# A pooled and RWKV-7 mixing block: the diagonal blocks of the score matrices gathered by ScalarE, chunk by chunk, and transposed by one contiguous VectorE instruction in place of two strided ones

## The chip, the cores and the metric

The kernel runs on one core of a Trainium2 chip. The metric is the device time of one execution in microseconds (us), taken as the median of several runs. The engines of the core are named as the profile names them: PE is TensorE (matmuls; PEld are its weight loads), DVE is VectorE, ACT is ScalarE, POOL is GpSimd, SP issues DMAs.

## The reference

`x` is (1, 4096, 1024), and everything is float32. Cut to what matters here:

```
h  = rmsnorm(x) * (1 + scale) + shift               # adaLN from c @ w_ada
p  = h @ w_in                                       # one projection for both branches
pool branch: trailing-window means (2, 4, 8, 16) minus the token, a small matmul, a SiLU gate
RWKV-7 branch, 512 channels, 8 heads of 64: r, w, k, v, a, z from p, each mixed with the token before
    kk = l2-normalised k * k_k
    S_t = S_{t-1} (diag(decay_t) - kk_t^T (a_t * kk_t)) + v_t^T k_t ;  y_t = S_t r_t
    y = groupnorm(y) + bonus, times a SiLU gate
out = rmsnorm(x + gate * (concat(pool, rwkv) @ w_out))
```

The recurrence over 4096 tokens is computed in chunks of 64 tokens. Within a chunk the state update of all tokens at once needs the inverse of a unit triangular 64x64 matrix, for each head.

## The kernel before, in words

Phase 1 (the first 440 us) computes the modulation, `h` and the pool branch. Phase 2 has 16 blocks, b = 0 to 15, of 256 tokens: 4 chunks (NCH) of 64 tokens times 8 heads (NH) make 32 instances (NI) of the triangular problem per block. For each block the program runs three functions:

- `scores(b)`: per chunk `ch`, PE multiplies BK with AR into two PSUM tiles (L659), and DVE multiplies these with a mask into `sc` (L666). `sc` is 128 partitions x 32 instances x 128 floats, so that the same element of two neighbouring instances lies 128 floats (512 bytes) apart.
- `inverse(b)`: the 64x64 matrix of each instance has two 32x32 blocks on its diagonal (rows 0 to 31 and rows 32 to 63). Both are brought with the instance in the partition and inverted there for all 32 instances at once. L703 transposes them into `Ab` (partitions 0 to 63), L704 multiplies by the norms `d2T`, L705 copies to partitions 64 to 127 (ACT), L707 copies to `W`; then come 30 back-substitution steps of two DVE instructions each, `Wt` = W * Ab (L721) and W += Wt (L726); L737 multiplies by `d2T` again ("W*d2T"); two transpositions (L739) write the result into `MT`, which is the lower 64 partitions of the tile `UV`; L740 transposes a part into `MQ` (DVE), L741 copies another (ACT). Then PE makes the off-diagonal block of the inverse: the products `qp` (L750), copies of them (L752), and a second set of products (L758). All DVE steps named here stand in `tc.high_priority(offset=PRI)`.
- `chain(b)`: the four chunks one after the other with the state S; L833 (`Sd`) is its first DVE instruction.

`front(b+1)` is the next block's projection: 17 segments named lo, then kS, rS, vS, zS for each of four pairs of heads. A segment is 8 times three matmuls into a PSUM tile `pj` (L552 to L554; f16 weights and activations in a high and a low part), an ACT eviction (L556) and a DVE eviction (L557). Between the segments lie small steps: `pl` and `pa` (L583, L584) with the activations `tw` and `ta`, the scan `L` (L591), `vps` (L624, copied by ACT into UV, L630) and `pb` (L637, used by DVE as `bon`, L638). `pj`, `pl`, `pa`, `vps` and `pb` share one pool of three PSUM banks in turn: each waits until what used its bank three allocations before has been read. `front` is a generator; `fill(n)` runs n of its steps at the places where `scores`, `inverse` and `chain` call it, so PE has the projection's matmuls among the others. In block 15 there is no next block, and from its inverse on `fill` runs `project`, the output projection (`po`, L947 to L949).

The Tile framework orders the instructions of each engine by priority and by its own estimates; each engine then executes its own list in order, and an instruction that waits holds up all that stand behind it. Some matmuls are pinned to program order.

Of the kernel before, what the change touches and what calls it, by code (L numbers as in the profile page):

```python
# [24 lines left out]
NH = 8  # L25
# [27 lines left out]
def kernel(  # L53
# [29 lines left out]
    V, A, G, PE, SP = nc.vector, nc.scalar, nc.gpsimd, nc.tensor, nc.sync  # L83
# [56 lines left out]
    with ExitStack() as ph:  # L140
# [179 lines left out]
        for tok in plan.split():  # L320
            op, q = tok[0], int(tok[1:] or 0)
# [158 lines left out]
    with ExitStack() as ph:  # L480
# [165 lines left out]
        def scores(b, f, fill):  # L646
            AR, BK = f["AR"], f["BK"]

            d2 = sm.tile([64, NI], F32, tag="d2", name=f"d2_{b}")
            d2T = sm.tile([P, 32], F32, tag="d2T", name=f"d2T{b}")  # L650
            sc = blk.tile([P, NI, P], F32, tag="sc", name=f"sc{b}")
            BT = blk.tile([P, NCH, 512], F32, tag="BT", name=f"BT{b}")
            for ch in range(NCH):

                pts = [pool.tile([P, 512], F32, tag=tg, name=f"scp{b}_{ch}_{tg}") for pool, tg in ((ps_sc, "sc"), (ps_x, "px"))]
                for j in range(4):
                    for hq in range(2):
                        o = 64 * hq
                        PE.matmul(  # L659
                            pts[hq][:, j * P : (j + 1) * P],  # L660
                            BK[o : o + 64, j, ch].rearrange("q a t -> q (a t)"),
                            AR[o : o + 64, j, ch].rearrange("q a t -> q (a t)"),
                            start=True, stop=True,
                        )
                for hq in range(2):
                    V.tensor_mul(  # L666
                        sc[:, ch * NH : (ch + 1) * NH, :].rearrange("q (j h) t -> q j h t", h=2)[:, :, hq],
                        pts[hq].rearrange("q (j t) -> q j t", j=4),
                        mask.unsqueeze(1).to_broadcast([P, 4, P]),
                    )  # L670
                fill(FS + 1)
                if ch == 2:
                    pt = ps_sc.tile([P, 512], F32, tag="sc", name=f"d2p{b}")
                    for c_ in range(NCH):
                        PE.transpose(pt[:64, c_ * P : (c_ + 1) * P], ssb[:, c_ * C : (c_ + 1) * C], ident)
                    V.tensor_scalar_max(
                        d2.rearrange("q (c p h) -> q c p h", c=NCH, h=2),
                        pt[:64].rearrange("q (c p e) -> q c p e", c=NCH, e=32)[:, :, :, 0:2], L2_EPS * L2_EPS,
                    )
                    V.reciprocal(d2, d2)  # L680
                    for g in range(2):
                        V.transpose(d2T[64 * g : 64 * g + 64], d2)
                if ch in (0, 3):
                    f["todo"].pop(0)()
                fill(FS)
                if ch % 2 == 0:
                    run(gns[0], 1)
            f["sc"], f["BT"], f["d2T"] = sc, BT, d2T

        def inverse(b, f, fill):  # L690

            fi = iter(FI)
            sc, d2T = f["sc"], f["d2T"]
            MT = f["UV"][0:64].rearrange("q c (h t) -> q (c h) t", h=NH)

            Ab = blk.tile([P, 32, 32], F32, tag="Ab", name=f"Ab{b}")
            W = blk.tile([P, 16, 32], F32, tag="W", name=f"W{b}")
            with tc.high_priority(offset=PRI):  # L700
                for kb in range(2):
                    o = 32 * kb
                    V.transpose(Ab[o : o + 32], sc[o : o + 32, :, o : o + 32].rearrange("s i t -> s t i"))  # L703
                V.tensor_mul(Ab[0:64], Ab[0:64], d2T[0:64].unsqueeze(2).to_broadcast([64, 32, 32]))  # L704
                A.copy(Ab[64:128], Ab[0:64])  # L705
                for g in range(2):
                    V.tensor_copy(W[64 * g : 64 * g + 64], Ab[0:64].rearrange("q (t g) s -> q t g s", g=2)[:, :, g, :])  # L707
            fill(next(fi))
            BK, BT = f["BK"], f["BT"]
            for ch in range(NCH):  # L710
                pt = ps_sc.tile([P, 512], F32, tag="sc", name=f"btp{b}_{ch}")
                for p in range(NPAIR):
                    PE.transpose(pt[:, p * P : (p + 1) * P], BK[:, p, ch].rearrange("q a t -> q (a t)"), ident)
                A.copy(BT[:, ch, :], pt)
                fill(FE)
            for k in range(30, 0, -1):
                r0 = (k + 1) // 2
                n = 16 - r0
                tmp = blk.tile([P, 16, 32], F32, tag="Wt", name=f"Wt{b}_{k}")
                with tc.high_priority(offset=PRI):  # L720
                    V.tensor_mul(  # L721
                        tmp[:, :n, :k],
                        W[:, r0:, k : k + 1].to_broadcast([P, n, k]),
                        Ab[:, k : k + 1, :k].to_broadcast([P, n, k]),
                    )
                    V.tensor_add(W[:, r0:, :k], W[:, r0:, :k], tmp[:, :n, :k])  # L726
                if k % 2 == 0:
                    fill(next(fi))
            Wf = W.rearrange("q t c -> q (t c)")
            MQ = blk.tile([P, NI, 32], F32, tag="Ab", name=f"MQ{b}")  # L730
            with tc.high_priority(offset=PRI):
                for kb in range(2):
                    for g in range(2):
                        q0 = 64 * g + 32 * kb
                        o = Wf[q0 : q0 + 32, g : g + 1]
                        G.memset(bass.AP(tensor=o.tensor, offset=o.offset, ap=[list(o.ap)[0], [34, 16]]), 1.0)
                V.tensor_mul(W, W, d2T.unsqueeze(1).to_broadcast([P, 16, 32]))  # L737
                for g in range(2):
                    V.transpose(MT[:, :, 0:32].rearrange("c i (t g) -> c g t i", g=2)[:, g], W[64 * g : 64 * g + 64])  # L739
                V.transpose(MQ[0:32], MT[0:32, :, 0:32])  # L740
                A.copy(MT[32:64, :, 32:64], MT[32:64, :, 0:32])  # L741
                G.memset(MT[32:64, :, 0:32], 0.0)
            fill(FT)
            f["px"] = [ps_x.tile([P, 512], F32, tag="px", name=f"px{b}_{hf}") for hf in range(2)]
            run(lead(b, f, 0))
            pt = ps_sc.tile([P, 512], F32, tag="sc", name=f"qp{b}")
            for j in range(8):
                for q in range(4):
                    i = 8 * q + j
                    PE.matmul(pt[32 * q : 32 * q + 32, j * 32 : (j + 1) * 32], sc[0:32, i, 32:64], MQ[0:32, i, :], start=True, stop=True)  # L750
            for q in range(4):
                A.copy(MQ[32:64, 8 * q : 8 * q + 8, :], pt[32 * q : 32 * q + 32, 0:256].rearrange("t (i c) -> t i c", c=32))  # L752
            fill(FQ)
            pt = ps_sc.tile([P, 512], F32, tag="sc", name=f"m21p{b}")
            for j in range(8):
                for q in range(4):
                    i = 8 * q + j
                    PE.matmul(pt[32 * q : 32 * q + 32, j * 32 : (j + 1) * 32], MQ[32:64, i, :], MT[32:64, i, 32:64], start=True, stop=True)  # L758
            for q in range(4):
                A.copy(MT[0:32, 8 * q : 8 * q + 8, 32:64], pt[32 * q : 32 * q + 32, 0:256].rearrange("c (i t) -> c i t", t=32))  # L760
# [3 lines left out]
        def ordered(mm):  # L764

            pin[0] = True
            return tc.keep_in_program_order(mm)
# [22 lines left out]
        def chain(b, f, fill):  # L790
            AR, UV, sc, BT, pc = f["AR"], f["UV"], f["sc"], f["BT"], f["pc"]
            MT = UV[0:64].rearrange("q c (h t) -> q (c h) t", h=NH)
            pe, po = f["px"]
            uo = 4 * HS
            for ch in range(NCH):
# [39 lines left out]
                for h in range(NH):  # L835
                    o, e = 64 * (h % 2), slice(h * HS, (h + 1) * HS)
                    ordered(PE.matmul(
                        psn[o : o + 64, (h // 2) * HS : (h // 2 + 1) * HS], BT[:, ch, e], UV[:, ch, e],
                        start=True, stop=True, skip_group_check=True,
# [70 lines left out]
        def run(g, n=100000):  # L910
            for _ in range(n):
                if next(g, run) is run:
                    return
# [51 lines left out]
        for b in range(NB2):  # L965
            f = fs[b]
# [80 lines left out]
```

## Time and profile before

| | |
|---|---|
| median of 3 runs | 2123.24 us (2123.21 to 2123.97) |
| the profiled execution | 2123.65 us, of which its span is 2121.9 us |
| TensorE clock granted, mean of the span | 0.982 of full |
| busy: PE, DVE, ACT, POOL | 1984.5, 1449.5, 965.5, 131.6 us |
| share of the chain that ended last: PE, DVE, ACT | 54%, 28%, 11% |

The busy time of an engine is what it spends in its own instructions. The chain that ended last is followed back from the last instruction to what released each step; its shares say on which engine the time to the end went.

### The profile page before, as it was taken

How to read it: one execution, taken by the hardware profiler on the slowest of the kernel's cores; microseconds unless marked ns; L12 is line 12 of the kernel's file. 1: busy time of each engine (PE TensorE's matmuls, PEld its weight loads, DVE VectorE, ACT ScalarE, POOL GpSimd, SP SyncE). 2: the span in 40 equal slices, each digit the busy share in tenths (PEclk: the TensorE clock that was granted, in tenths of full speed). 3: DMA queues.
4: the chain of work that ended last, by engine and by line, in shares of the span. 5: the costliest groups of instructions: out<-in, count | busy, mean ns of one | idle time of the engine just before them, and what ended most of it. 6: DMA issues, size and time to landing. Idle time of an engine off the chain costs nothing.

```text
span 2121.9 us, 48336 instructions
## 1 busy us (share of the span) xinstructions
PE 1984.5 (94%) x20186; PEld 1463.6 (69%) x20186; DVE 1449.5 (68%) x3549; ACT 965.5 (46%) x2119; POOL 131.6 (6%) x262
## 2 busy tenths in 40 slices
PE   5999999999999999999999999999999989999998
PEld 2444444677777777777777777777777767788886
DVE  7898987566857768578577686786776866533333
ACT  3545433345455554554555545545555453312111
POOL 0000000000000000000000100000000000100000
PEclk8999999999999999999999999999999999999999
DMA  8867767200110110101101101011011434443431
GB/s 304 278 224 239 243 217 269 66 21 2 31 27 7 31 26 7 32 2 31 27 7 31 27 6 32 2 31 27 6 32 27 134 111 140 157 142 130 153 105 70
DMA packets 140445, 183.19 MB, mean 86 GB/s; under 512 B 12098, under 2 KB 94018, under 8 KB 140227
## 3 DMA queue, kind: packets, MB, share of 16 engines
q1 hardware_dynamic: 140226, 180.11, 26.0%
q8 instruction: 158, 2.59, 0.5%
q14 instruction: 61, 0.49, 0.1%
HBM read 121.22 MB, written 58.85 MB: 85 GB/s over the span
## 4 chain that ended last, share of the span: by engine, by line
PE 54%; DVE 28%; ACT 11%; issue 4%; DMA 2%; POOL 0%; SPq 0%; DVEq 0%; ACTq 0%; POOLq 0%
PE po L947 6%; PE po L949 5%; PE po L948 5%; PE pj L552 5%; PE pj L554 4%; PE pj L553 4%; DVE W L726 4%; DVE Wt L721 4%; PE pp L412 4%; PE pp L411 4%; PE pp L410 4%; DVE Ab L703 3%; PE psn L821 2%; PE scp_sc L659 2%; PE px L809 2%
## 5 line engine op out<-in xcount | busy, mean ns | idle before, releaser
L552 PE MATMUL pj<-hh,w2h 128*128 128x257 f16 x2176 | 609.5, 280 | 48.2 <-DVE bon L638 24.0
L554 PE MATMUL pj<-hh,w2l 128*128 128x257 f16 x2176 | 604.1, 278 | 0.0
L553 PE MATMUL pj<-hl,w2h 128*128 128x257 f16 x2176 | 602.3, 277 | 0.0
L553 PEld LDWEIGHTS <-w2h 128*128 128x128 f16 x2176 | 217.5, 100 | 87.4 <-issue 57.4
L552 PEld LDWEIGHTS <-w2h 128*128 128x128 f16 x2176 | 214.9, 99 | 52.2 <-issue 6.5
L554 PEld LDWEIGHTS <-w2l 128*128 128x128 f16 x2176 | 213.5, 98 | 34.1
L947 PE MATMUL po<-wo,mh 128*128 128x512 f32 x512 | 204.3, 399 | 3.7 <-ACT mh L931 3.7
L948 PE MATMUL po<-wo,mh 128*128 128x512 f32 x512 | 201.8, 394 | 0.0
L411 PE MATMUL pp<-lo,w1h 128*128 128x512 f16 x512 | 194.0, 379 | 1.4 <-DVE lo L225 1.4
L410 PE MATMUL pp<-hi,w1h 128*128 128x512 f16 x512 | 194.1, 380 | 1.1 <-ACT hi L224 1.1
L412 PE MATMUL pp<-hi,w1l 128*128 128x512 f16 x512 | 194.0, 379 | 0.0
L951 DVE TENSOR_TENSOR x<-po,x 128x512 f32<-128x512 f32 x64 | 44.2, 690 | 151.9 <-PE po L949 151.9
L953 ACT ACTIVATE sq<-x 128x512 f32<-128x512 f32 x64 | 40.4, 631 | 208.8 <-DVE x L951 190.6
L721 DVE TENSOR_TENSOR Wt<-W,Ab 128x30 f32<-128x30 f32 (+7 forms) x480 | 117.5, 245 | 10.2
L726 DVE TENSOR_TENSOR W<-W,Wt 128x30 f32<-128x30 f32 (+7 forms) x480 | 117.5, 245 | 9.1
L947 PEld LDWEIGHTS po<-wo,mh 128*128 128x128 f32 x512 | 96.7, 189 | 25.9 <-ACT mh L931 3.9
L948 PEld LDWEIGHTS po<-wo,mh 128*128 128x128 f32 x512 | 96.6, 189 | 22.3
L949 PE MATMUL po<-wo,ml 128*128 128x512 f32 x256 | 101.4, 397 | 0.0
L557 DVE SCALAR_TENSOR_TENSOR kS<-pj,c,kS 128x256 f32<-128x256 f32 x64 | 30.6, 478 | 100.2 <-ACT kS L556 100.2
L412 PEld LDWEIGHTS <-w1l 128*128 128x128 f16 x512 | 50.1, 98 | 61.6 <-issue 2.0
L411 PEld LDWEIGHTS <-w1h 128*128 128x128 f16 x512 | 50.1, 98 | 59.4 <-issue 1.2
L410 PEld LDWEIGHTS <-w1h 128*128 128x128 f16 x512 | 50.2, 98 | 59.0 <-issue 0.8
(243 smaller groups left out, 3814.0 us busy)
## 6 DMA issues: line engine op xcount, KB each, us to landing
x<-in_x_dram SPq DMA_DIRECT2D x64, 256.0 KB, 3.0
out_dram<-x SPq DMA_DIRECT2D x64, 256.0 KB, 2.1
xk<-in_xT_dram SPq DMA_DIRECT2D x56, 256.0 KB, 4.1
xt<-in_x_dram SPq DMA_DIRECT2D x28, 512.0 KB, 5.7
wada<-in_w_ada_dram SPq DMA_DIRECT2D x24, 512.0 KB, 5.7
w2raw<-in_w_in_dram SPq DMA_DIRECT2D x17, 512.0 KB, 5.4
hh<-hT_hi SPq DMA_DIRECT2D x32, 257.0 KB, 3.6
hl<-hT_lo SPq DMA_DIRECT2D x32, 257.0 KB, 3.0
```

The lines of the kernel that those rows point to most:

```text
L410: PE.matmul(pp, w1_hi[m][:, k, :], hi, start=(k == 0), stop=False)
L411: PE.matmul(pp, w1_hi[m][:, k, :], lo, start=False, stop=False)
L412: PE.matmul(pp, w1_lo[m][:, k, :], hi, start=False, stop=(k == KT - 1))
L552: unpin(PE.matmul(pp, w2_hi[m][:, k, :], hh[k], start=(k == 0), stop=False))
L553: PE.matmul(pp, w2_hi[m][:, k, :], hl[k], start=False, stop=False)
L554: PE.matmul(pp, w2_lo[m][:, k, :], hh[k], start=False, stop=(k == KT - 1))
L703: V.transpose(Ab[o : o + 32], sc[o : o + 32, :, o : o + 32].rearrange("s i t -> s t i"))
L721: V.tensor_mul(tmp[:, :n, :k], W[:, r0:, k : k + 1].to_broadcast([P, n, k]), Ab[:, k : k + 1, :k].to_broadcast([P, n, k]),)
L726: V.tensor_add(W[:, r0:, :k], W[:, r0:, :k], tmp[:, :n, :k])
L947: unpin(PE.matmul(po, mh[:, k, ts_], wo[0][k][n], start=(k == 0), stop=False))
L948: PE.matmul(po, mh[:, k, ts_], wo[1][k][n], start=False, stop=False)
L949: PE.matmul(po, (ml[:, k] if b % 2 == 0 else ml[k])[:, ts_], wo[0][k][n], start=False, stop=(k == KT - 1))
```

## The change

In `scores`, after the mask multiplies of each chunk, ACT copies the two 32x32 diagonal blocks of the chunk's eight instances into a staging area `stg`: 32 partitions, 32 columns t, 8 instances, with the instances innermost. `stg` is the first 1024 floats of partitions 0 to 63 of the block's `UV`, which are free until L739 writes `MT` there. In `inverse`, one DVE transposition of 64 partitions x 1024 contiguous floats reads `stg`, in place of two of 32 x 1024 that read `sc` with a hop of 512 bytes from element to element. The values in `Ab` are the same. From here on line numbers of the changed kernel are larger: L660 is L659, L667 is L666, the new copies are L675, the transposition is L706, and all lines behind it are 3 higher (L707 is L704, L753 is L750).

```
     def scores(b, f, fill):
...
+            stg = f["stg"] = f["UV"][0:64].rearrange("q c e -> q (c e)")[:, 0:1024].rearrange("q (t i) -> q t i", t=32)
             for ch in range(NCH):
...
                         mask.unsqueeze(1).to_broadcast([P, 4, P]),
                     )
+
+                for kb in range(2):
+                    o, i8 = 32 * kb, slice(ch * NH, (ch + 1) * NH)
+                    A.copy(stg[o : o + 32, :, i8], sc[o : o + 32, i8, o : o + 32].rearrange("q i t -> q t i"))
                 fill(FS + 1)
...
     def inverse(b, f, fill):
...
             with tc.high_priority(offset=PRI):
-                for kb in range(2):
-                    o = 32 * kb
-                    V.transpose(Ab[o : o + 32], sc[o : o + 32, :, o : o + 32].rearrange("s i t -> s t i"))
+                V.transpose(Ab[0:64], f["stg"])
                 V.tensor_mul(Ab[0:64], Ab[0:64], d2T[0:64].unsqueeze(2).to_broadcast([64, 32, 32]))
```

With it the order of other instructions changes. The places below are of block 5; blocks 1 to 14 read alike. A row of the order is the engine's list of instructions: a running number, the line, the operation, what it writes and reads with the buffer's number, and the shape; "x2" stands for two alike.

DVE, at the head of the inverse, from the last mask multiply of the scores to the first back-substitution step (`Wt_30`), before:

```order
1407 L666 TENSOR_TENSOR sc_10345<-scp_3_px,mask 128x4x128
1408 L557 SCALAR_TENSOR_TENSOR kS_1_10495<-pj_1_10424,c_103,kS_1_10495 128x256
1409 L703 STREAM_TRANSPOSE Ab_10516<-sc_10345 32x1024 x2
1410 L638 TENSOR_TENSOR bon_9158<-pb_3_10507,vS_15_10234 128x256
1411 L704 TENSOR_TENSOR Ab_10516<-Ab_10516,d2T_10344 64x1024
1412 L557 SCALAR_TENSOR_TENSOR rS_2_10536<-pj_2_10500,c_103,rS_2_10536 128x256
1413 L707 COPY W_10517<-Ab_10516 64x512 x2
1414 L591 SCALAR_TENSOR_TENSOR L_0_10548<-rst,tw_0_10543 128x256
1415 L721 TENSOR_TENSOR Wt_30_10617<-W_10517,Ab_10516 128x30
```

DVE at the same place after the change:

```order
1407 L667 TENSOR_TENSOR sc_10380<-scp_3_px,mask 128x4x128
1408 L557 SCALAR_TENSOR_TENSOR kS_1_10538<-pj_1_10463,c_103,kS_1_10538 128x256
1409 L638 TENSOR_TENSOR bon_9188<-pb_3_10550,vS_15_10269 128x256
1410 L706 STREAM_TRANSPOSE Ab_10559<-UV_9191 64x1024
1411 L557 SCALAR_TENSOR_TENSOR rS_2_10578<-pj_2_10543,c_103,rS_2_10578 128x256
1412 L707 TENSOR_TENSOR Ab_10559<-Ab_10559,d2T_10379 64x1024
1413 L591 SCALAR_TENSOR_TENSOR L_0_10590<-rst,tw_0_10585 128x256
1414 L710 COPY W_10560<-Ab_10559 64x512 x2
1415 L724 TENSOR_TENSOR Wt_30_10659<-W_10560,Ab_10559 128x30
```

`bon` has moved ahead of the transposition, one transposition stands where two stood, and the eviction rS and the scan L have each moved one place up.

PE, at the tail of the inverse, where the projection of the third pair of heads (`pl_2`, `pa_2`), the `vps` of the second pair and the next segment `pj_11` stand, before:

```order
9638 L554 MATMUL pj_10_10903<-hh_1_10363,w2l_1767 128x257
9639 L583 MATMUL pl_2_10937<-lo_0_10420,up 128x256
9640 L584 MATMUL pa_2_10938<-lo_0_10420,up 128x256
9641 L624 MATMUL vps_1_10951<-cmat,vS_7_10795 128x128 x2
9642 L552 LDWEIGHTS w2h_1770
9643 L552 MATMUL pj_11_10962<-hh_0_10359,w2h_1770 128x257
```

PE at the same place after the change:

```order
9636 L554 MATMUL pj_10_10945<-hh_1_10400,w2l_1767 128x257
9637 L583 MATMUL pl_2_10979<-lo_0_10459,up 128x256
9638 L584 MATMUL pa_2_10980<-lo_0_10459,up 128x256
9639 L753 MATMUL qp_11101<-MQ_11020,sc_10380 32x32 x9
9640 L624 MATMUL vps_1_10993<-cmat,vS_7_10837 128x128 x2
9641 L552 LDWEIGHTS w2h_1770
9642 L552 MATMUL pj_11_11004<-hh_0_10396,w2h_1770 128x257
```

Nine of the 32 `qp` products, which read `MQ`, have moved ahead of `vps_1`. Before the change blocks 1 to 14 have none there and block 0 has nine; after it blocks 1 to 14 have nine and block 0 has four.

ACT at the same place, with the copy of MT (L741, L744 after the change; it reads and writes UV) and the evictions and activations of the third pair, before:

```order
743 L577 ACTIVATE sq_2_10895<-kS_9_10892,vec 128x256
744 L556 ACTIVATE rS_10_10934<-pj_10_10903,c_102 128x256
745 L586 ACTIVATE tw_2_10941<-pl_2_10937,pv 128x256
746 L588 ACTIVATE ta_2_10943<-pa_2_10938,pv 128x256
747 L741 COPY UV_9161<-UV_9161 32x32x32
748 L589 ACTIVATE tw_2_10941<-tw_2_10941,one 128x256
749 L630 COPY UV_10371<-vps_1_10951 64x2x128 x2
```

ACT at the same place after the change:

```order
767 L577 ACTIVATE sq_2_10937<-kS_9_10934,vec 128x256
768 L744 COPY UV_9191<-UV_9191 32x32x32
769 L556 ACTIVATE rS_10_10976<-pj_10_10945,c_102 128x256
770 L586 ACTIVATE tw_2_10983<-pl_2_10979,pv 128x256
771 L588 ACTIVATE ta_2_10985<-pa_2_10980,pv 128x256
772 L589 ACTIVATE tw_2_10983<-tw_2_10983,one 128x256
773 L630 COPY UV_10408<-vps_1_10993 64x2x128 x2
```

The copy of MT has moved ahead of the eviction rS and of tw and ta. On DVE at this place the eviction kS of the third pair, which stood ahead of the last two back-substitution steps, now stands behind W*d2T, and Sd and rS have each moved one place down, behind the transpositions into UV and into MQ.

## Rows read from the trace of the kernel before

**Rows 1.** The page: busy time of PE and DVE with their share of the span and their instructions, and the chain that ended last, by engine and by line.

```profile
PE 1984.5 (94%) x20186; PEld 1463.6 (69%) x20186; DVE 1449.5 (68%) x3549; ACT 965.5 (46%) x2119; POOL 131.6 (6%) x262
...
PE 54%; DVE 28%; ACT 11%; issue 4%; DMA 2%; POOL 0%; SPq 0%; DVEq 0%; ACTq 0%; POOLq 0%
PE po L947 6%; PE po L949 5%; PE po L948 5%; PE pj L552 5%; PE pj L554 4%; PE pj L553 4%; DVE W L726 4%; DVE Wt L721 4%; PE pp L412 4%; PE pp L411 4%; PE pp L410 4%; DVE Ab L703 3%; PE psn L821 2%; PE scp_sc L659 2%; PE px L809 2%
```

**Rows 2.** Busy time by stretch, from one block's first L703 to the next block's: blocks 0, 1, 4, 5 and 13. Columns: from and to in us from the span's start, length, then busy us (instructions) of PE, PEld, DVE, ACT and POOL, the granted TensorE clock (1.00 is full), the busy share of the DMA engines, GB/s.

```profile
463.98:553.07 89.09, 82.49 (x1078) 65.83 (x1075) 61.84 (x169) 45.29 (x107) 5.81 (x11) 0.96 0.06 16
553.07:637.82 84.75, 78.91 (x1063) 62.90 (x1060) 61.49 (x170) 45.01 (x107) 6.05 (x11) 0.98 0.08 21
807.59:891.65 84.06, 77.53 (x1063) 61.91 (x1060) 61.40 (x170) 44.88 (x107) 6.06 (x11) 1.00 0.08 21
891.65:976.61 84.96, 78.92 (x1063) 62.82 (x1060) 61.38 (x169) 45.13 (x107) 6.05 (x11) 0.98 0.08 20
1569.72:1654.63 84.91, 78.94 (x1063) 62.63 (x1060) 61.49 (x170) 45.01 (x107) 6.06 (x11) 0.98 0.11 33
```

**Rows 3.** The groups of instructions by line and shape: three transpositions on DVE and a copy on ACT. Columns: out<-in, partitions x elements and type, count, then busy us, mean ns of one, and the engine's idle us ahead of them with its releaser.

```profile
L703 DVE STREAM_TRANSPOSE Ab<-sc 32x1024 f32<-32x1024 f32 x32 | 61.6, 1927 | 0.2
L739 DVE STREAM_TRANSPOSE UV<-W 64x512 f32<-64x512 f32 x32 | 33.7, 1053 | 0.2
L740 DVE STREAM_TRANSPOSE MQ<-UV 32x1024 f32<-32x1024 f32 x16 | 19.6, 1223 | 0.8 <-ACT sq L953 0.8
L752 ACT COPY MQ<-qp 32x256 f32<-32x256 f32 x64 | 23.3, 364 | 1.6
```

**Rows 4.** The timeline of DVE at the head of the inverse of block 5. Columns: start, duration, engine, line, operation, and in brackets idle time ahead with its releaser where there was any.

```profile
890.65 0.68 DVE L666 TENSOR_TENSOR sc<-scp_px,mask 128x512 f32<-128x512 f32 x1
...
891.65 3.87 DVE L703 STREAM_TRANSPOSE Ab<-sc 32x1024 f32<-32x1024 f32 x2
895.54 0.42 DVE L638 TENSOR_TENSOR bon<-pb,vS 128x256 f32<-128x256 f32 x1
895.88 1.21 DVE L704 TENSOR_TENSOR Ab<-Ab,d2T 64x1024 f32<-64x1024 f32 x1
897.02 0.47 DVE L557 SCALAR_TENSOR_TENSOR rS<-pj,c,rS 128x256 f32<-128x256 f32 x1
897.41 0.84 DVE L707 COPY W<-Ab 64x512 f32<-64x512 f32 x2
898.29 0.69 DVE L591 TENSOR_TENSOR_SCAN L<-rst,tw 128x256 f32<-128x256 f32 x1
898.89 0.17 DVE L721 TENSOR_TENSOR Wt<-W,Ab 128x30 f32<-128x30 f32 x1
```

**Rows 5.** The group of the projection's first matmul of each three, with PE's idle time ahead of it by releaser.

```profile
L552 PE MATMUL pj<-hh,w2h 128*128 128x257 f16 x2176 | 609.5, 280 | 48.2 <-DVE bon L638 24.0 <-DVE rS L557 12.4 <-ACT UV L630 10.4
```

**Rows 6.** The scores of block 5: busy time of the stretch (columns as in rows 2), and, of ACT's timeline in it, the row with the longest idle time ahead.

```profile
876.60:891.33 14.73, 14.73 (x154) 12.14 (x154) 9.85 (x21) 5.51 (x14) 1.64 (x1) 1.00 0.19 49
...
887.31 1.50 ACT L886 ACTIVATE mx<-ytp,pv 128x128 f32<-128x128 f32 x4 [2.95 <-PE ytp L884]
```

**Rows 7.** DVE's timeline: W*d2T in blocks 1, 4 and 14, the first, the fourth and the last of the 14 middle blocks. The L703 of blocks 1 and 4 start at the left ends of their stretches in rows 2, and that of block 14 at the right end of the last stretch there.

```profile
584.82 0.69 DVE L737 TENSOR_TENSOR W<-W,d2T 128x512 f32<-128x512 f32 x1
838.64 0.69 DVE L737 TENSOR_TENSOR W<-W,d2T 128x512 f32<-128x512 f32 x1
1686.53 0.69 DVE L737 TENSOR_TENSOR W<-W,d2T 128x512 f32<-128x512 f32 x1
```

**Rows 8.** The tail of the inverse of block 5, timelines of DVE (W*d2T and the transposition into MQ), and PE (the first matmul of the pj group that stands behind pb).

```profile
923.61 0.69 DVE L737 TENSOR_TENSOR W<-W,d2T 128x512 f32<-128x512 f32 x1
...
927.10 1.22 DVE L740 STREAM_TRANSPOSE MQ<-UV 32x1024 f32<-32x1024 f32 x1
...
929.10 0.27 PE L552 MATMUL pj<-hh,w2h 128*128 128x257 f16 x1 [1.14 <-ACT UV L630]
```

**Rows 9.** The same place in block 0: timelines of DVE, ACT (the copy of MT) and PE (the qp products, and the pj group that stands behind pb).

```profile
495.76 0.69 DVE L737 TENSOR_TENSOR W<-W,d2T 128x512 f32<-128x512 f32 x1
...
499.20 1.23 DVE L740 STREAM_TRANSPOSE MQ<-UV 32x1024 f32<-32x1024 f32 x1
...
498.86 1.04 ACT L741 COPY UV<-UV 32x1024 f32<-32x1024 f32 x1 [1.48 <-DVE UV L739]
...
500.48 0.52 PE L750 MATMUL qp<-MQ,sc 32*32 32x32 f32 x18 [2.89 <-DVE MQ L740]
...
505.89 0.27 PE L552 MATMUL pj<-hh,w2h 128*128 128x257 f16 x1
```

**Rows 10.** Two stretches in which the granted clock was half: in block 0 behind the qp products' wait, and in block 5 behind the wait for `bon`. Columns as in rows 2.

```profile
500.40:503.70 3.30, 3.22 (x31) 2.58 (x32) 1.49 (x4) 2.59 (x8) 0.70 (x2) 0.50 0.00 0
896.20:899.60 3.40, 3.40 (x18) 2.67 (x17) 3.20 (x8) 1.14 (x2) 0.24 (x2) 0.50 0.02 5
```

**Rows 11.** Block 15, timelines of ACT (the cast of the output projection's first input) and of PE (the first matmul of the output projection).

```profile
1738.47 1.04 ACT L931 CAST mh<-mk 128x1024 fp32r<-128x1024 f32 x1 [1.94 <-DMA mk<-mixp]
...
1739.57 0.80 PE L947 MATMUL po<-wo,mh 128*128 128x512 f32 x1 [3.66 <-ACT mh L931]
```

More of the change, by code (lines that the diff above doesn't have):

```diff
@@ L652, in scores @@
             BT = blk.tile([P, NCH, 512], F32, tag="BT", name=f"BT{b}")
+            stg = f["stg"] = f["UV"][0:64].rearrange("q c e -> q (c e)")[:, 0:1024].rearrange("q (t i) -> q t i", t=32)
             for ch in range(NCH):
@@ L670, in scores @@
                     )
+                for kb in range(2):
+                    o, i8 = 32 * kb, slice(ch * NH, (ch + 1) * NH)
+                    A.copy(stg[o : o + 32, :, i8], sc[o : o + 32, i8, o : o + 32].rearrange("q i t -> q t i"))
                 fill(FS + 1)
@@ L700, in inverse @@
             with tc.high_priority(offset=PRI):
-                for kb in range(2):
-                    o = 32 * kb
-                    V.transpose(Ab[o : o + 32], sc[o : o + 32, :, o : o + 32].rearrange("s i t -> s t i"))
+                V.transpose(Ab[0:64], f["stg"])
                 V.tensor_mul(Ab[0:64], Ab[0:64], d2T[0:64].unsqueeze(2).to_broadcast([64, 32, 32]))
```

## The prediction

> **What bounds the kernel now.** I read the page first: TensorE is busy for 94% of the span, but the chain that ended last runs 54% on PE and 28% on VectorE, so PE's wait for DVE counts somewhere, and "Ab L703", the two transpositions that the change replaces, has 3% of the chain by itself [rows 1]. That fits a simple count: 32 of them at 1927 ns are 61.6 us [rows 3], 2.9% of the span.
>
> The busy time by block says where the wait is. Phase 2 has 16 blocks; b=1 to 14 (the "middle blocks") each last 84 to 85 us from one block's first transposition to the next one's, with PE busy for about 79 [rows 2]. I call the start of a block's L703 T. From T on, DVE goes through the inverse without a gap: in the head of block 5 every row starts where the last one ends [rows 4]. PE in that time does the next block's projection and waits for PSUM banks that DVE or ACT empties: 24.0 us over 14 blocks for `bon`, which stands behind the transpositions on DVE (1.7 each), 12.4 for rS and 10.4 for the copy into UV (about 0.8 and 0.7 each) [rows 5]. So inside the inverse DVE sets the pace; once M is made, PE's own work does. A gain in the inverse arrives at the end only if PE can go on when the inverse is done, so the tail of the inverse has to be read as closely as its head.
>
> [...]
>
> **The change, part by part: the head.** The old head is in [rows 4]: the first back-substitution step starts at T+7.24. In the new order `bon` comes ahead of the transposition, and a chunk's two ACT copies must follow its mask multiplies. The last multiply ends at T-0.32 (890.65+0.68). Then come two copies of 32x256. No ScalarE copy in the trace reads with a hop from element to element. Lower bound: L752, the same shape, 0.364 us. Upper bound: 0.364 plus 256 times what the hop costs DVE per element, (1927-1223)/1024 ns, which makes 0.54 [rows 3]. I take a start at T-0.27, 0.42 from first to second and 0.50 for the second (nearer the upper end, for the hop is the same 512 bytes): T+0.65. `bon` (0.34 from start to start) lies beside them. The one contiguous transposition of 64x1024: 1.22 by L740, 32x1024 contiguous, if 64 partitions cost what 32 do; upper bound 2.1, since L739's 64x512 take 1.05 each [rows 3]. I take 1.22, as L703 and L740 show the price to go with the elements of a partition and their order: T+1.9. Behind it stand rS 0.39, the multiply 1.14, the scan L 0.60 and the copies of W 0.88, all from start to start in [rows 4]: the first step starts at T+4.9, **2.3 us earlier**.
>
> The hop itself is not gone, it is moved to ScalarE. The row: with equal shapes DVE pays 0.69 ns per element for it [rows 3]. [...]
>
> **The other copies.** Of 8 per block six are hidden: in the 14.73 us of the scores ACT is busy for 5.51 and the longest idle piece is 2.95 us ahead of L886 [rows 6]; three pairs add 2.8 us there. Without that cover each pair would delay an eviction by 0.9. In total ACT gets some 60 us more work, and DVE 42 less (61.6 to 16 x 1.22); neither is an end in itself.
>
> **To the end of the steps.** W*d2T (L737) starts 31.75 us after T in the first middle block and 31.90 in the last, 31.74 in the mean of 14; in block 4, without the fall of the clock, 31.05 [rows 2, 7]. The new head takes the 1.7 us `bon` stall away, after which many of the falls come, so I start from 31.05: less 2.3, less 0.3 (in the new order the eviction kS of the next pair stands behind W*d2T instead of ahead of the last step; 0.39 by the same form, part of which hid a latency) = 28.4. That is **3.3 earlier** than the mean.
>
> **The tail.** Here the order changes more than the diff tells. Before, PE has the projection's vps and the next pj group ahead of the first qp product, so it works on while DVE transposes; in the middle blocks after, nine qp products stand ahead of vps. They need MQ, the last transposition of the inverse, and PE takes its instructions in order: everything of the projection waits behind them. On ACT the copy of MT (L741) moves ahead of the rS eviction, tw, and ta, which then wait for DVE's transpositions as well. The kernel before has this order in one place, block 0, and so shows its price. There W*d2T starts at 495.76, MQ is done at 500.43, PE stands for 2.89 us ahead of qp, the clock is at half for the next 3.3 us, and the pj group behind pb starts at 505.89: 10.1 after W*d2T [rows 9, 10]. In block 5, in the old order, the same group starts 5.5 after W*d2T (929.10-923.61), with one wait of 1.14 [rows 8]. The difference is 4.6; the nine products, done here, are spared later (0.52 us at half clock, 0.2 or so at full): **4.4 later**. About 1.5 of it is the clock: 3.3 us at half speed with PE busy for 3.22 [rows 10].
>
> **Sum.** A middle block: -3.3 + 4.4 = +1.1; nothing behind the tail changes order enough to give it back, since PE has work for nearly all of what is left. Times 14: +15.4. The clock did not fall in 2 of 14 blocks now; if it stays up in as many after, 2 x 1.5 comes off: -3.0. Block 0 has the old tail already (its stall 2.89) and gains the head only: -2.3, and 0.3 for kS: -2.6. Block 15 has no next projection; there PE waits 3.66 us for a cast that waits for a DMA, not for the inverse [rows 11]: 0. Total +9.8, against the profiled execution's own 2123.65 us (span 2121.9): **2133.5**; the median of the runs is 0.4 below that execution, so 2133.
>
> **Rivals.**
> *A, the forecast (0.62).* With the lower bound of the copies (-0.2 each block) and a tail smaller by 0.3, 2126; with their upper bound and a tail 0.8 larger, 2147. That is its own range.
> *B, the clock stays up behind the new stall (0.15).* Then 1.5 comes off in the other 12 blocks as well: 2133.5-18 = 2115.5, slightly faster than before. For it: blocks 4 and 10 stalled for 1.7 us without a fall. Against it: behind the longer stalls, 2.89 in block 0 and 3.66 in block 15, it fell both times.
> *C, MQ is there when PE comes to qp (0.05).* Then the head's gain goes through: 14 x -3.3 - 2.6 = -49, so 2075, far on the other side. It decides itself at PE's arrival: MQ would have to come 2.9 us earlier against PE than in block 0. The head gives DVE 3.3, but it gives PE the `bon` stall back too, so most of that is a wash.
> *D, a step costs its upper bound (0.13).* If 64 partitions make the transposition 2.1 us, each of 15 blocks loses 0.9: 2133.5+13 = 2147. Or the clock falls a second time per block, at the rS stall in the inverse, 0.7 x 14: 2143.
> The rest (0.05) is what I don't see, either way.
>
> **How the numbers follow.** A measurement of this kernel tells some 0.2%, 4.2 us, from no change: 2119.0 to 2127.5 is the same. The lower edge of A (0.10), a little of B (0.02) and of the rest (0.03) lie there: same 0.15. Faster: B 0.13, C 0.05: 0.18. Slower: A 0.52, D 0.13, the rest 0.02: 0.67. The range takes in B and both halves of D with a little room: 2114 to 2150; C and the rest stay outside.
>
> **What would show it.** In the changed kernel's profile: 16 transpositions of 64x1024 near 1.2 us (2.1: D); 128 copies of 0.36 to 0.54; no idle time of PE with `bon` as releaser; the first step 4.9 after T's counterpart (the end of kS's eviction) and W*d2T at 28.4; qp with MQ as releaser, idle 2.5 to 4 us each time, some 40 to 50 in total where it was 2.9; a fall of the clock behind it (none: B); a middle block of 85.7 to 86. I am wrong in the head if copies or handover take over 1.3 us, and wrong in the tail if PE does not stand at qp, or if a later wait that I count as staying (rS, UV) goes with it.

## The result, and the profile after

The changed kernel takes 2145.07 us (2144.45 to 2146.44), the kernel before, on the same chip, 2123.22 (2122.79 to 2123.97). The ratio is 1.0103, with a 95% interval from 1.0086 to 1.0121: **slower by 21.8 us**. The forecast had the sign and, in the main, the mechanism, but less than half of the size (9.8); the time lies in the upper part of its range (2114 to 2150).

The page of the profiled execution (2144.86 us, span 2143.2), busy time and the chain that ended last, against [rows 1]:

```profile
PE 1995.0 (93%) x20186; PEld 1473.1 (69%) x20186; DVE 1410.0 (66%) x3533; ACT 1039.2 (48%) x2247; POOL 131.9 (6%) x262
...
PE 58%; DVE 27%; ACT 9%; issue 3%; DMA 2%; SPq 1%; POOL 0%; DVEq 0%; ACTq 0%; POOLq 0%
```

DVE got 39 us less work and ACT 74 more. PE's busy time rose by 10.5 us with the same 20186 instructions, while the mean granted clock fell from 0.982 to 0.977; PE's idle time (span less busy time) rose by 10.8, from 137.4 to 148.2. The windows of blocks 0, 4 and 5, from one block's transposition to the next one's, columns as in [rows 2]:

```profile
462.35:548.93 86.58, 80.56 (x1072) 63.70 (x1070) 59.13 (x168) 49.69 (x116) 5.87 (x11) 0.98 0.07 18
808.49:894.50 86.01, 79.14 (x1061) 63.15 (x1060) 59.03 (x168) 49.62 (x116) 6.08 (x11) 0.98 0.08 20
894.50:981.85 87.35, 80.47 (x1061) 63.85 (x1060) 59.02 (x167) 49.62 (x116) 6.08 (x11) 0.96 0.08 20
```

The middle blocks up to b=13 last 86.0 to 86.1 us or, every third one (b=2, 5, 8, 11), 87.3 to 87.4, with a clock of 0.96; they were 84.1 to 85.0. The last one, b=14, which the prediction counts among the blocks of 84 to 85 us, is shorter in both kernels (80.8 before).

Block 0 is 2.5 us shorter, as forecast, but not by the forecast's way. Its wait of 2.89 us for MQ, which was to stay, has shrunk to 0.44. In its place PE now waits ahead of `pa`, for the eviction kS that stands behind W*d2T in the new order; and half speed comes there all the same (a granted clock of 0.50 from 496.2 to 499.5 us):

```profile
493.60 0.70 PE L584 MATMUL pa<-lo,up 64*128 64x256 f32 x2 [1.18 <-DVE kS L557]
494.74 0.26 PE L753 MATMUL qp<-MQ,sc 32*32 32x32 f32 x8 [0.44 <-DVE MQ L743]
```

The groups by line and shape that the change touches: the transposition, the copies, PE's first matmul of each three, its transposes of BK (`btp`), and the qp products. The number behind the second bar is the engine's idle time ahead of the group, in us.

```profile
L706 DVE STREAM_TRANSPOSE Ab<-UV 64x1024 f32<-64x1024 f32 x16 | 19.8, 1236 | 10.2 <-ACT UV L675 10.2
...
L675 ACT COPY UV<-sc 32x256 f32<-32x256 f32 x128 | 80.8, 631 | 63.5 <-DVE sc L667 62.8
...
L552 PE MATMUL pj<-hh,w2h 128*128 128x257 f16 x2176 | 612.5, 281 | 18.8 <-DVE rS L557 9.5 <-ACT tw L586 8.5 <-ACT up L425 0.8
...
L716 PE MATMUL btp<-ident,BK 128*128 128x128 f32 x256 | 40.1, 280 | 14.4 <-ACT BT L717 13.3 <-ACT mx L889 1.1
...
L753 PE MATMUL qp<-MQ,sc 32*32 32x32 f32 x1024 | 16.7, 202 | 40.9 <-DVE MQ L743 40.9
```

The 24.0 us behind `bon` and the 10.4 behind UV are gone [rows 5], and 40.9 us behind MQ, where there were 2.9 in all, have come: 2.9 in each of 14 blocks. What `bon` gave back in the head did not stay free, either: PE now waits there for ACT, 8.5 us in all for tw and 13.3 for the copies BT (0.2 before). The kernel with the copy of MT on POOL, below, has both of these too, so they are not what makes the difference.

The head of block 5, DVE's timeline, to hold against [rows 4]:

```profile
892.47 0.68 DVE L667 TENSOR_TENSOR sc<-scp_px,mask 128x512 f32<-128x512 f32 x1
893.07 0.47 DVE L557 SCALAR_TENSOR_TENSOR kS<-pj,c,kS 128x256 f32<-128x256 f32 x1
893.47 0.41 DVE L638 TENSOR_TENSOR bon<-pb,vS 128x256 f32<-128x256 f32 x1
894.50 1.24 DVE L706 STREAM_TRANSPOSE Ab<-UV 64x1024 f32<-64x1024 f32 x1 [0.62 <-ACT UV L675]
...
898.69 0.19 DVE L724 TENSOR_TENSOR Wt<-W,Ab 128x30 f32<-128x30 f32 x1
```

T's counterpart, the start of the row behind kS, is 893.47. The transposition starts 1.03 later, having waited for the second copy, and the first step comes at T+5.2 (T+7.2 before). The tail, timelines of DVE (W*d2T) and PE (the qp products and the pj group behind pb): first two rows of block 4, then block 5, to hold against [rows 8].

```profile
836.03 0.69 DVE L740 TENSOR_TENSOR W<-W,d2T 128x512 f32<-128x512 f32 x1
...
846.29 0.27 PE L552 MATMUL pj<-hh,w2h 128*128 128x257 f16 x1
```

```profile
922.04 0.69 DVE L740 TENSOR_TENSOR W<-W,d2T 128x512 f32<-128x512 f32 x1
...
926.77 0.52 PE L753 MATMUL qp<-MQ,sc 32*32 32x32 f32 x18 [2.89 <-DVE MQ L743]
...
933.64 0.27 PE L552 MATMUL pj<-hh,w2h 128*128 128x257 f16 x1
```

In block 5 W*d2T starts at T+28.57 (31.96 before); the pj group behind pb comes 11.6 us after it (5.5 before), and 10.3 after it in block 4. And the clock: two windows behind the qp wait, in block 4 and in block 5.

```profile
840.90:844.20 3.30, 3.30 (x32) 2.59 (x29) 1.54 (x4) 2.36 (x7) 0.72 (x2) 0.50 0.00 0
926.40:933.00 6.60, 6.23 (x45) 4.68 (x46) 3.83 (x9) 3.47 (x9) 1.23 (x2) 0.50 0.00 0
```

In block 4 half speed (a granted clock of 0.50) lasts some 3.3 us, in block 5 twice as long.

### The profile page after: what moved, and what is told of

It is laid out like the page before. It is cut to its first block, busy times and chain, and to the rows that moved or that the text cites. A ratio compares the mean times of both kernels' runs of the same rounds, so it can differ in the third digit from the quotient of the medians.

```text
span 2143.2 us, 48435 instructions
## 1 busy us (share of the span) xinstructions
PE 1995.0 (93%) x20186; PEld 1473.1 (69%) x20186; DVE 1410.0 (66%) x3533; ACT 1039.2 (48%) x2247; POOL 131.9 (6%) x262
## 4 chain that ended last, share of the span: by engine, by line
PE 58%; DVE 27%; ACT 9%; issue 3%; DMA 2%; SPq 1%; POOL 0%; DVEq 0%; ACTq 0%; POOLq 0%
PE po L950 6%; PE pj L552 6%; PE po L952 5%; PE po L951 5%; PE pj L553 5%; PE pj L554 5%; DVE W L729 5%; DVE Wt L724 4%; PE pp L412 4%; PE pp L410 4%; PE pp L411 4%; PE psn L824 2%; PE scp_sc L660 2%; PE px L812 2%; PE vps L624 2%
## 5 line engine op out<-in xcount | busy, mean ns | idle before, releaser
L552 PEld LDWEIGHTS <-w2h 128*128 128x128 f16 x2176 | 216.4, 99 | 53.4 <-issue 6.5
L675 ACT COPY UV<-sc 32x256 f32<-32x256 f32 x128 | 80.8, 631 | 63.5 <-DVE sc L667 62.8
L410 PEld LDWEIGHTS <-w1h 128*128 128x128 f16 x512 | 50.2, 98 | 58.9 <-issue 0.8
```

The lines of the kernel that those rows point to most:

```text
L410: PE.matmul(pp, w1_hi[m][:, k, :], hi, start=(k == 0), stop=False)
L552: unpin(PE.matmul(pp, w2_hi[m][:, k, :], hh[k], start=(k == 0), stop=False))
L675: A.copy(stg[o : o + 32, :, i8], sc[o : o + 32, i8, o : o + 32].rearrange("q i t -> q t i"))
```

## The experiments

Two theories stood against each other. "Order": the contiguous transposition gains what it should, and the loss is in the tail, where ACT's copy of MT and nine qp products have moved ahead of the projection's work. "Copies": 128 copies of 0.63 us on ACT are what costs. T is used as before, and T+28.6 stands for 28.6 us after T; "the idle time" is PE's, as the groups by line give it.

**The copy of MT moved to POOL.** In the changed kernel:

```
-                A.copy(MT[32:64, :, 32:64], MT[32:64, :, 0:32])
+                G.tensor_copy(MT[32:64, :, 32:64], MT[32:64, :, 0:32])
```

> The changed kernel with one line moved: the copy of MT (L744) is issued by POOL and no longer by ACT. Nothing else is edited; in the order of blocks 1 to 14 the eviction rS, tw and ta no longer stand behind that copy, vps stands ahead of the qp products as in the kernel before, and all 32 qp products stand behind the first products of the chain. Theory 'order' (the loss is in the tail: ACT's copy of MT ahead of rS, tw and ta, and nine qp products ahead of vps): W*d2T stays at 28.6 us after T, the idle time with MQ as releaser goes (2.89 a block), the stretch at half clock behind it too, a middle block takes 81.5 to 83 us in place of 86.0 to 87.4, and the whole 2080 to 2100 us, well under both kernels. Rival 'copies' (the 128 copies on ACT, 0.63 us each, are what costs): no gain, 2140 to 2148. Rival 'POOL' (POOL's copy is slow or slows DVE): the gain is cut, 2105 to 2130, and DVE's transpositions beside it take longer than 1.03 and 1.23.

Measured: 2082.19 us, ratio 0.9805 (0.9789 to 0.9822), 41 us under the kernel before and 63 under the changed one. A middle block (b=2), and the groups of the qp products and the copy on POOL:

```profile
630.43:712.39 81.96, 77.42 (x1063) 62.01 (x1060) 58.65 (x169) 48.41 (x115) 7.37 (x12) 1.00 0.08 21
```

```profile
L753 PE MATMUL qp<-MQ,sc 32*32 32x32 f32 x1024 | 12.3, 194 | 0.4 <-DVE MQ L743 0.4
...
L744 POOL COPY UV<-UV 32x1024 f32<-32x1024 f32 x16 | 20.0, 1252 | 57.8 <-DVE UV L742 57.8
```

W*d2T still starts at T+28.57, the granted clock is 1.00 in the mean of blocks 1 to 13 (548.45 to 1613.00 us), and the copies are all there. From W*d2T to the next block's T it takes 53.4 us, where the changed kernel takes 57.5 and the kernel before 53.0. So "copies" is refuted as the cause, and the gain of the head is real once the tail lets it through. POOL takes 1.25 us for what ACT did in 1.04, with nobody waiting, and DVE's transpositions beside it last 1.05 and 1.23 us as before: the rival 'POOL' is out.

**The qp products late, the copy still on ACT.**

```
-                    PE.matmul(pt[32 * q : 32 * q + 32, j * 32 : (j + 1) * 32], sc[0:32, i, 32:64], MQ[0:32, i, :], start=True, stop=True)
+                    ordered(PE.matmul(pt[32 * q : 32 * q + 32, j * 32 : (j + 1) * 32], sc[0:32, i, 32:64], MQ[0:32, i, :], start=True, stop=True))
```

> The changed kernel with the qp products pinned behind the first products of the chain, so that vps stands behind pa again; ACT's copy of MT stays ahead of rS, tw and ta. It tells the two halves of the tail's order apart. If the nine qp products are the cause, their 2.89 us of waiting go: 2100 to 2110. If the copy's slot on ACT is, PE only waits elsewhere, at vps, for a tw that stands behind the copy (it is ready 33.5 us after T, and qp's wait ended at 33.3): 2142 to 2149, with some 3.3 us of idle time ahead of vps per block. I expect the second.

Measured: 2148.84 us, 1.0124 (1.0109 to 1.0139). The group of vps, and its row in block 4 (the blocks last 86.0 and 87.3 as in the changed kernel):

```profile
L624 PE MATMUL vps<-cmat,vS 128*128 128x128 f32 x256 | 49.1, 320 | 64.1 <-ACT tw L586 64.1
```

```profile
847.60 1.22 PE L624 MATMUL vps<-cmat,vS 128*128 128x128 f32 x4 [3.23 <-ACT tw L586]
```

PE stands 3.2 us in place of 2.9, one group of instructions on; the rest of the 64.1 is in other, shorter waits of vps, which were there before. Of the two moves that the prediction priced together, the slot of ACT's copy ahead of rS and tw is thus enough to make the wait without the qp products. The reverse was not tried: no run has nine qp products ahead of vps in a middle block with the copy off ACT. They could not have started sooner, for MQ is ready no earlier with the copy on POOL: in block 0 of that kernel four qp products stand ahead of vps and start 4.77 us after W*d2T, in the changed kernel they start 4.73 after it. The copy on POOL did away with both moves at once.

**The same wait, filled.** In the changed kernel, with eight more matmuls behind `pa`; with them the qp products stand late without a pin.

```
-                pl, pa = (ps_pj.tile([P, TB2], F32, tag="pj", name=f"{n}{b}_{p}") for n in ("pl", "pa"))
+                pl = ps_pj.tile([P, TB2], F32, tag="pj", name=f"pl{b}_{p}")
+                pw = ps_pj.tile([P, 512], F32, tag="pj", name=f"pa{b}_{p}")
+                pa = pw[:, 0:TB2]
...
+                for _ in range(8 if p == 2 and b > 0 else 0):
+                    PE.matmul(pw[:, TB2:512], up[64:128, ps_], lo[64:128], start=True, stop=True)
```

> As the kernel with the qp products pinned late, and eight more matmuls of 64x128 by 64x256 behind pa of the third pair in each block from b=1 on, into unused columns of its PSUM bank; nobody reads them. They take some 2.6 us in which PE would otherwise stand, and change no wait of another engine. It prices the clock: if the stretch at half speed (3.4 us in 10 of 15 blocks, 6.7 in 5) comes from PE's standing, it goes, and 1.7 to 3.1 us a block with it: 2110 to 2120. If the clock falls whatever PE does there, or if what the clock costs is hidden: 2142 to 2150, as without the matmuls.

Measured: 2122.10 us, 0.9996 (0.9987 to 1.0005), 26.7 under the kernel without the filling. A middle block (b=2), then the group of the eight matmuls and that of vps:

```profile
636.33:720.92 84.59, 80.61 (x1079) 64.89 (x1076) 59.08 (x169) 49.67 (x116) 6.08 (x11) 1.00 0.08 20
```

```profile
L588 PE MATMUL pa<-lo,up 64*128 64x256 f32 x240 | 55.8, 384 | 0.0
...
L628 PE MATMUL vps<-cmat,vS 128*128 128x128 f32 x256 | 44.5, 297 | 17.7 <-ACT tw L590 17.7
```

This takes the tail's price apart. The middle blocks b=1 to 13 average 86.45 us in the changed kernel (86.54 with the qp products late), 84.6 filled, and 81.98 with the copy on POOL: the clock costs 1.9 us a block, and the waiting itself, with whatever else the move to POOL changes, 2.6. By length of the half-speed stretch the clock's price is 1.4 us in the blocks of 86.0 and 2.7 in those of 87.3. I had expected 2110 to 2120. The filling does harm in block 0, which it makes 4 us longer (90.45): there PE has already stood 1.2 us ahead of `pa`, for kS, and the granted clock is 0.50 for 6.7 us:

```profile
496.00:502.70 6.70, 6.70 (x24) 4.72 (x24) 3.10 (x7) 2.52 (x6) 0.43 (x1) 0.50 0.00 0
```

Without these 4 us the time would lie inside what I expected.

**The copies alone.** The new copies, with the strided transpositions and nobody reading the copies:

```
-                V.transpose(Ab[0:64], f["stg"])
+                for kb in range(2):
+                    o = 32 * kb
+                    V.transpose(Ab[o : o + 32], sc[o : o + 32, :, o : o + 32].rearrange("s i t -> s t i"))
```

> The copies of the change are made, but the two strided transpositions of the kernel before read sc as they did, and nobody reads the copies. The order of the rest is that of the kernel before (vps ahead of qp, MT's copy behind rS, tw and ta). Theory 'order': the copies lie in ACT's idle time or beside the 3.9 us of the transpositions, 2121 to 2127. Rival 'copies': most of the loss is there, 2138 to 2146.

Measured: 2124.61 us, 1.0001 (0.9992 to 1.0011). The copies and the waits of the projection:

```profile
L675 ACT COPY UV<-sc 32x256 f32<-32x256 f32 x128 | 80.9, 632 | 63.5 <-DVE sc L667 62.8
...
L552 PE MATMUL pj<-hh,w2h 128*128 128x257 f16 x2176 | 609.7, 280 | 37.9 <-DVE rS L557 14.6 <-DVE bon L638 12.3 <-ACT UV L630 9.6
```

81 us of ACT work cost nothing that can be measured in the whole: in the middle blocks they lie in ACT's idle time, as the prediction had it. (In block 15 they do cost something, as the sum below tells.)

**The copy of MT on POOL in the kernel before**, by the same line as in the first experiment.

> The kernel before, with the copy of MT (L741) issued by POOL and no longer by ACT; the strided transpositions stay and no staging copies are made. With it and the changed kernel with the same edit, the two edits are told apart. Theory: the copy holds tw's second half and the UV copies back in the old order too, which PE feels as the 1.14 us ahead of the pj group behind pb; this goes, the 1.7 us for bon and the falls of the clock behind it stay: a middle block takes 83.5 to 84 us (84.8 now), the whole 2104 to 2112, so that of the 41 us that the changed kernel with the POOL copy gains on the kernel before some 15 are the copy's and some 25 the change's. Rival: the copy's slot is worth nothing in the old order (2119 to 2127), and all the gain is the change's once its tail is free; or all the gain is the copy's (2080 to 2090).

Measured: 2124.21 us, 1.0006 (0.9996 to 1.0015): no gain, and my expectation was wrong. The projection's waits, then the windows of block 5 and of two stretches in it, and a row of PE's timeline there; last, ACT's timeline in block 1, with the copies of qp, in the kernel before and in this one (W*d2T starts at 584.82 and 583.23):

```profile
L552 PE MATMUL pj<-hh,w2h 128*128 128x257 f16 x2176 | 613.4, 282 | 36.3 <-DVE bon L638 23.8 <-DVE rS L557 11.1 <-ACT up L425 0.8
```

```profile
890.73:976.06 85.33, 79.91 (x1063) 63.45 (x1060) 61.27 (x170) 43.70 (x106) 7.07 (x12) 0.96 0.08 20
895.00:897.10 2.10, 2.02 (x10) 1.43 (x10) 2.09 (x5) 0.91 (x1) 0.00 (x0) 0.50 0.03 8
935.60:939.00 3.40, 3.40 (x44) 2.35 (x44) 0.00 (x0) 1.92 (x6) 0.00 (x0) 0.51 0.00 0
...
933.16 0.93 PE L758 MATMUL m21p<-UV,MQ 32*32 32x32 f32 x6 [0.82 <-ACT MQ L752]
```

```profile
594.53 0.42 ACT L618 ACTIVATE tz<-zS 128x256 f32<-128x256 f32 x1 [0.89 <-DVE zS L557]
594.97 1.53 ACT L752 COPY MQ<-qp 32x256 f32<-32x256 f32 x4
...
592.85 0.42 ACT L618 ACTIVATE tz<-zS 128x256 f32<-128x256 f32 x1 [1.31 <-DVE zS L557]
593.29 1.53 ACT L752 COPY MQ<-qp 32x256 f32<-32x256 f32 x4
```

The 10.4 us behind UV are indeed gone [rows 5], and PE comes to the qp products 0.5 us earlier or more. But their copies on ACT stand behind `tz`, which comes no earlier, so they start 10.07 us after W*d2T where it was 10.15, and what hangs on them gains no more than that: blocks 1 and 2 take 84.7 to 84.8 us, hardly less than before. Blocks 4 and 5, with a mean clock of 0.96, take 85.3; block 5 has two stretches at half clock, the old one behind `bon` and a new one that begins some 2.4 us behind the wait of 0.8 for the copies of qp. From the mean clock of the span, 0.972 where it was 0.982, I estimate some 12 stretches of 3.4 us more than before (0.010 of 2126.7 us, at 1.7 us each), so most of the later blocks have a second one. Block 0, which had the wait for MQ, loses it and lasts 84.0 in place of 89.1; that and the longer middle blocks about balance. The `bon` wait, 23.8, stays. So neither edit gains alone (the POOL copy gains nothing, the change loses 22), and the two together gain 41: W*d2T comes 3.2 us earlier, the way from there to the next T is 0.4 longer than before, and in the middle blocks the clock stays up.

**The copies in another order**, which walks the instances outside and the columns inside:

```
-                    A.copy(stg[o : o + 32, :, i8], sc[o : o + 32, i8, o : o + 32].rearrange("q i t -> q t i"))
+                    A.copy(stg[o : o + 32, :, i8].rearrange("q t i -> q i t"), sc[o : o + 32, i8, o : o + 32])
```

> The changed kernel with the staging copies walking the same elements in another order: 32 contiguous floats of an instance are read and written 32 floats apart, in place of reading with a hop of 512 bytes per element and writing in runs of 8. If only hops on the reading side cost ACT, a copy takes 0.36 to 0.40 us in place of 0.63 and the head 0.5 less, which passes through PE's wait for MQ: 0.5 a block, 2135 to 2140. If a hop on the writing side costs the same, 0.6 or more and no change: 2142 to 2148.

> The changed kernel with the copy of MT on POOL, and the staging copies in runs of 32 read and 32 floats apart written. With MT's copy on POOL PE no longer waits for MQ, so that half a us less in the head shows only in its remaining waits for DVE in the inverse (rS, 0.6 a block): 2074 to 2082, against 2082 without the runs.

Measured: 2149.35 us, 1.0126 (1.0111 to 1.0141), and with MT's copy on POOL 2081.65, 0.9808 (0.9793 to 0.9822), the same as with the first order of walking. The first is a little above what I expected; its middle blocks average 86.42 us, as in the changed kernel, and in its profile phase 2 only begins later, which the sum below takes up. **And with a contiguous read**, which leaves the gathering out:

```
+                    A.copy(stg[o : o + 32, :, i8], sc[o : o + 32, ch * NH : ch * NH + 2, :].rearrange("q a (t i) -> q (a t) i", i=8))
```

> The changed kernel with the staging copies reading 256 contiguous floats of the chunk's first two instances in place of the diagonal blocks, written as before in runs of 8: the gathering is left out, only the duration of a copy is looked at. If the hop on the reading side is what makes a copy 0.63 us, it takes 0.36 to 0.40; if the runs of 8 on the writing side are, it stays at 0.6.

Measured: 2136.72 us, in one run, so without an interval. The group of the copies, first of the kernel that writes with the hop, then of the one that reads contiguously, with its qp products:

```profile
L675 ACT COPY UV<-sc 32x256 f32<-32x256 f32 x128 | 81.1, 633 | 63.5 <-DVE sc L667 62.7
```

```profile
L675 ACT COPY UV<-sc 32x256 f32<-32x256 f32 x128 | 51.4, 402 | 70.9 <-DVE sc L667 70.1
...
L753 PE MATMUL qp<-MQ,sc 32*32 32x32 f32 x1024 | 16.1, 199 | 40.9 <-DVE MQ L743 40.9
```

A copy costs 0.40 us without a hop at each element and 0.63 with one, on whichever side it lies: the hop is (632-402)/256 = 0.90 ns per element on ACT, where it was 0.69 on DVE. The faster copies bring the head 0.46 us forward, and that passes through: most of the middle blocks last 85.6 in place of 86.0. PE's wait for MQ stays 2.9, because PE comes to it earlier as well. Two of the blocks (b=2 and 10) have the long stretch at half speed, behind the same wait; the mean granted clock of the span is 0.979 (0.977 in the changed kernel, with five).

## Why the prediction was right or wrong, point by point

**The head: right, but for the price of a copy.** 2.3 earlier was forecast for the first step and about 2.0 came (T+5.2 in place of 4.9), W*d2T at T+28.57 in place of 28.4. The transposition is 1.236 us for 64 partitions (1.22 assumed; D's 2.1 is refuted). The copies broke their upper bound, 0.63 against 0.54: I had applied DVE's price of the hop to ACT and taken 0.364 for the rest, which is a contiguous copy from PSUM, not one that writes in runs of 8. From the end of the last mask multiply to the transposition it takes 1.35 us, just over the 1.3 that the prediction set as its sign of a wrong head. The last experiments show what a hop costs ACT, on both sides: 0.63 us with a hop at each element of the reading or of the writing, 0.40 with neither.

**The other copies: right.** The scores, from the first mask multiply to the last, take as long as before (12.16 us), and the kernel with the copies alone takes no longer.

**The tail: right in place and size.** 4.4 later was forecast; in the blocks with the shorter half-speed stretch, W*d2T to the next T takes 57.4 to 57.6 us where it took 53.0, so 4.4 to 4.6 later. PE stands 2.9 us ahead of qp in each block from b=1 on and 40.9 in all, inside the 40 to 50 forecast. Which of the two moves does it I had not told apart: ACT's copy makes the wait without the other; whether the qp products would do so alone is not shown.

**The clock: the step that failed.** "if it stays up in as many after, 2 x 1.5 comes off: -3.0" was wrong twice. In the kernel before 12 of the 14 middle blocks have one stretch of 3.4 us at a granted clock of 0.50, and blocks 4 [rows 2] and 10 have none:

```profile
1316.06:1400.12 84.06, 77.30 (x1063) 61.78 (x1060) 61.41 (x169) 44.89 (x107) 6.05 (x11) 1.00 0.08 21
```

After the change the clock fell to 0.50 in every one of the 15 blocks, so the 3.0 must not come off; and in five of them half speed lasted 6.6 us in place of 3.3, which is 1.33 more in each of four blocks and 0.3 in b=14. The prediction took block 0's one stretch (1.5 us) as the price of every fall. That is right for a short stretch (1.4), but the stretch is not a constant: the filled kernel puts the clock at 1.9 us a block on average. These two, 3.0 and 5.6, are 8.6 of the 12.0 us by which the forecast fell short. Rival B, with the clock up, is refuted; rival D's second half, more time at half speed, came about, but as a longer stretch in the tail and not as a second one at rS.

**The sum.** To the 9.8 forecast come 2.4 for the head (14 x 0.17), 3.0 for the clock that did not stay up in two blocks, 5.6 for the long stretches, and 2.7 for block 15, where the prediction had put 0. In block 15 PE waits 1.1 us twice ahead of its transposes of BK, for ACT's mx and BT, which stand behind new copies, and 2.3 for the cast, where it had one wait of 3.7 [rows 11]; the half speed that sets in at that wait lasts 6.7 us where it was 3.4:

```profile
1753.88 1.09 PE L716 MATMUL btp<-ident,BK 128*128 128x128 f32 x8 [1.08 <-ACT mx L889]
...
1757.00 0.66 PE L716 MATMUL btp<-ident,BK 128*128 128x128 f32 x4 [1.13 <-ACT BT L717]
1759.98 0.80 PE L950 MATMUL po<-wo,mh 128*128 128x512 f32 x1 [2.33 <-ACT mh L934]
...
1759.10:1765.80 6.70, 5.82 (x14) 4.62 (x15) 6.02 (x19) 3.68 (x4) 0.25 (x2) 0.50 0.52 162
```

(The last stretch is counted in both kernels from 1.2 us behind the start of the last mask multiply, where T lies in the kernel before.) Phase 2 began 2.7 earlier. The change does not touch what lies ahead of it, and over the ten profiles, one of each kernel, that moment lies between 461.3 and 468.1, so I take this for scatter; that it just cancels block 15's share is chance. Together 20.8, against 21.2 between the two profiled executions. With the clock as it came the forecast would have been 18.4. Block 15's share is read off two profiles and was not tried by itself; in the other kernels with the copies that last stretch is 1.2 to 3.4 us longer than before, too. Block 0 came out as forecast (-2.5 for -2.6) by luck: the wait that was to stay there went, and another came.

**Rival C** (the gain passes through) needed MQ 2.9 us earlier against PE. The contiguous read shows that a faster head alone does not bring that: 0.46 us earlier, the same 2.9. With ACT's copy on POOL the gain did pass through.

## What to carry to other kernels

When an edit shortens one engine's chain, read the order that it makes elsewhere for places where an instruction now stands ahead of work that has nothing to do with it: here a 1.04 us copy, moved ahead of an eviction and two activations on ACT together with products that wait for the same step, made a loss of 22 us of what is a gain of 41 with the copy on POOL. A place in the old program that has the new order already gave a good price for the wait; for the clock it was only one draw. If such a copy can go to an engine with nothing to do, try that, and price it together with the edit: here neither gained without the other. (Leaving the copy on ACT, but behind the eviction and the activations, was not tried in the changed kernel.)

## What the runs showed of the hardware

In blocks 1 to 14 of the changed kernel a stall of PE of 2.9 us came with a granted clock of 0.50 every time. With the qp products late, where PE stands 3.2 us, the mean clock of blocks 3 and 4 is 0.98 and 0.96; with eight matmuls that nobody reads in the stall's place it is 1.00 over blocks 1 to 13. Where it came, half speed lasted 3.3 us or 6.6: in every third block of the changed kernel it was the longer, and with the contiguous read, behind the same 2.9 us, in two blocks of fourteen. What decides between the two these runs do not show. ACT's copy of 32x256 floats costs 0.23 us more with a hop at each element, be it 512 bytes on the reading side (0.632 us) or 128 on the writing side (0.633, against 0.402). The transposition of 1024 contiguous floats per partition took DVE 1.23 us for 32 partitions and 1.24 for 64.
